# Experts of a two-layer trunk: order of the full-column products, a tenth weight block, and a pool for the first mixer's constants

## The chip, the cores and the metric

One core of one Trainium2 chip. The metric is the device time of one execution, in microseconds (us). The kernel before took 1505.41 us (median of 3 runs, 1500.89 to 1505.77).

## What is computed

Two layers over 512 tokens of width 1024, all in float32. Each has a mixer and then a mixture of 16 experts, in which every expert takes the 64 tokens with the highest affinity. Cut to what matters here:

```python
for layer in range(DEPTH):                     # DEPTH = 2; mixer 0: attention + pooling, mixer 1: gated convolution
    ...
    h_lat = _post_norm(h_lat, m_lat[2] * y_lat, ln_mix_g[layer], ln_mix_b[layer])
    f_lat = _expert_choice_ffn(_modulate(h_lat, m_lat[3], m_lat[4]), w_router[layer],
                               w_exp_gate[layer], w_exp_up[layer], w_exp_down[layer])
    h_lat = _post_norm(h_lat, m_lat[5] * f_lat, ln_ffn_g[layer], ln_ffn_b[layer])

def _expert_choice_ffn(u, w_router, w_g, w_u, w_d):    # u: (1, 512, 1024), 16 experts
    b, n, _ = u.shape
    cap = CAPACITY_FACTOR * n // N_EXPERTS             # 64 rows per expert
    logits = jnp.einsum('bnd,de->ben', u, w_router, preferred_element_type=jnp.float32)
    aff = jax.nn.softmax(logits, axis=1)
    gate, idx = lax.top_k(aff, cap)
    bidx = jnp.arange(b)[:, None, None]
    xe = u[bidx, idx]
    hg = jnp.einsum('becd,edf->becf', xe, w_g)         # w_g, w_u, w_d: (16, 1024, 1024) float32 per layer
    hu = jnp.einsum('becd,edf->becf', xe, w_u)
    ye = jnp.einsum('becf,efd->becd', jax.nn.silu(hg) * hu, w_d) * gate[..., None].astype(u.dtype)
    return jnp.zeros_like(u).at[bidx, idx].add(ye)
```

The weights of the experts are 2 x 16 x 3 matrices of 4 MB, 403 MB, which are read from HBM once.

## The kernel before

The order of every engine's instructions is the order of the Python code; nothing reorders it.

**Weight blocks.** A weight block is a tile of 128 partitions x 16 KB (2 MB, half a matrix). There are eight in the pool `base` (tags B0 to B7) and, while experts run, a ninth in a pool of its own (`x8`, opened by `open_x8`, L831). `self.queue` lists all loads in the order of use. Whenever a step has read a block for the last time, `next_load(b)` (L213) pops the next item and issues its load into that block on SP's queue; the load waits there until the block's readers are done. In an expert 0 the blocks of the gate and up products are given back in halves (`next_half`, L226). Once the last down matrix of a layer has been popped, block 8 is not loaded again: it becomes `self.spare`, which holds two rows of layer-norm constants (`gb`, built by `ln_row`, L269, with 32 TensorE matmuls into `p_gb`).

**One expert** (L1335 to L1372). TensorE's stationary operand is 64 columns wide in the products, since an expert has 64 tokens, so two matmuls for the two halves of the 1024 outputs run side by side in the two column halves of the array (64x512 each; the profile calls them 128\*64). A product `p_g`, `p_u` or `p_d` is 32 of these (`product`, L1289, two weight blocks of 16). The other steps of TensorE use all 128 columns: `gather` (`p_ga`, L1277, 32 matmuls: a selection matrix times H collects half of the features for the next pair of experts), the four transposes of the hidden rows (`p_t`, L1359), one matmul for the next selection matrix (`p_sb`, L1309, 16 rows deep) and `scatter` (`p_sc`, L1327: two matmuls per tile of 128 tokens, then two VectorE operations that add them into the accumulator `A`, L1330). The scatter belongs to the expert before, and is placed so:

```python
p_g = product("g", ...)            # 64-column
scatters(0)                        # tiles 0 and 1 of the expert before: 4 matmuls
p_u = product("u", ..., lambda: scatters(2))   # tiles 2 and 3, between the two halves of up
gather(g, 4 * (e % 2), 4 * (e % 2) + 4)        # not in experts 14 and 15
p_t, hT; st = scatter_sel(e)       # transposes, their copy, p_sb
p_d = product("d", ...)
```

In expert 15 the two halves of the scatter are in the middle of gate and behind it, and its down product is another routine (`out_mm`, L1384). PSUM has four banks with the tag `sc`, and one each with `g`, `u`, `d` and `tr`; gather, scatter, `p_sb` and `p_gb` use `sc`, the transposes `tr`.

**Around it.** `cst` holds all constants (1025 columns), among them the rotary tables and two tables that the first mixer alone reads; `condp` the conditioning vector padded with zeros to 32 columns. `x_load` (L837) reads x into H near the end of attention, and `load_gates` (L415) reads two bias rows at the start of layer 1's mixer; both go through POOL's queue.

Of the kernel before, what the change touches and what calls it, by code (L numbers as in the profile page):

```python
# [51 lines left out]
NCONST = _const_layout()  # L52


def _const_array():
# [7 lines left out]
    put("tri", np.triu(np.ones((P, P))))  # L63
    t = np.arange(S)
# [5 lines left out]
    put("cos", np.concatenate([cos, cos], -1).reshape(TT, P, HD).transpose(1, 0, 2))  # L70
    put("sin", np.concatenate([-sin, sin], -1).reshape(TT, P, HD).transpose(1, 0, 2))
    put("iota", np.broadcast_to(np.arange(1, CAP + 1), (P, CAP)))
    put("slot1", (np.arange(P) % CAP) + 1)
    sb = np.zeros((P, P))
    sb[0::32] = 1
    put("selb", sb)
    iv = np.ones((4, 16))
# [5 lines left out]
    put("inv", np.broadcast_to(iv, (P, 4, 16)))  # L83
    return a
# [101 lines left out]
class Trunk:  # L186
# [127 lines left out]
    def mod_item(self, layer, i, misc, dve=False, pool=None, kp=0, bufs=2):  # L314
# [12 lines left out]
        def sums(k0, k1):  # L327
# [5 lines left out]
            for k in range(k0, k1):  # L333
                c = self.condp[:, k, 0:1]
# [12 lines left out]
        def both(i):  # L347
# [18 lines left out]
        def share(i):  # L366
# [10 lines left out]
            nc.gpsimd.tensor_tensor(W[:, i], W[:, i], self.condp[:, i, 0:1].to_broadcast([P, 512]), ALU.mult)  # L377
            c = self.condp[:, KH + i, 0:1]
# [8 lines left out]
        def second():  # L387
# [11 lines left out]
            sel = one.to_broadcast([P, P]) if dve else self.cv("selb")  # L399
# [15 lines left out]
    def load_gates(self, layer, m2b, eng=None):  # L415
# [4 lines left out]
        eng = eng or nc.gpsimd  # L420
# [15 lines left out]
    def run(self):  # L436
# [5 lines left out]
        self.condp = base.tile([P, KO, 32], F32, name="condp")  # L442
        self.identb = base.tile([NE, NE], BF16, name="identb")
# [42 lines left out]
    def layer0_mixer(self):  # L486
        nc, tc, ins, base = self.nc, self.tc, self.ins, self.base
        ident = self.cv("ident")
        with ExitStack() as st:
# [4 lines left out]
            wgrp = pool.tile([P, 4, P], F32, name="wgrp")  # L494
            identr = pool.tile([P, P], F32R, name="identr")
# [11 lines left out]
            with ExitStack() as s2:  # L507
# [30 lines left out]
                nc.sync.dma_start(self.cst, ins["cst"])  # L538
                nc.sync.dma_start(gq, ins["qkg"].broadcast_to([P, 2 * HD]))
# [13 lines left out]
                nc.gpsimd.tensor_copy(self.identb, self.cv("ident", NE)[:, 0:NE])  # L553
# [86 lines left out]
                cs = self.cv("cos").rearrange("p (t i) -> p t i", t=TT)  # L640
                sn = self.cv("sin").rearrange("p (t i) -> p t i", t=TT)
# [189 lines left out]
    def open_x8(self, layer):  # L831

        self.layer, self.spare, self.x8s = layer, None, ExitStack()
        self.x8 = self.x8s.enter_context(self.tc.tile_pool(name=f"x8_{layer}", bufs=1))
        self.next_load(8)

    def x_load(self):  # L837

        self.H = self.base.tile([P, TT, D], F32, tag="H", name="H")
        self.nc.gpsimd.dma_start(self.H, self.ins["x"])  # L840

    def attention(self, pool, ps, identr, kH, kL, v, pp, wgrp, qs, qm, ms, nmx, sm, ri, s_tile, pb_mm, pb_out, mod_steps):
# [14 lines left out]
        with tc.tile_pool(name="l0a", bufs=1) as wk:  # L857
# [16 lines left out]
            def pool_group(g):  # L874
# [12 lines left out]
                iv = self.cv("inv").rearrange("p (g i) -> p g i", g=4)[:, g]  # L887
# [305 lines left out]
    def topk(self, layer, aff, sp, free, steps):  # L1193
# [45 lines left out]
        nc.scalar.copy(self.slotb, pr)  # L1239
# [4 lines left out]
    def moe(self, layer):  # L1244
# [6 lines left out]
        with tc.tile_pool(name=f"ex{layer}", bufs=2) as wk:  # L1251
# [18 lines left out]
            def gather(g, j0, j1, e0=0, e1=2):  # L1270
# [3 lines left out]
                pg = self.bank(shape=(P, j1 - j0, n), name="p_ga")  # L1274
# [60 lines left out]
            for e in range(NE):  # L1335
# [10 lines left out]
                scatters(2 if e == NE - 1 else 0)  # L1346
# [3 lines left out]
                p_u = product("u", lambda k: xe[k // KH][:, k % KH, e % 2], f"u{layer}_{e}", None if e == NE - 1 else lambda: scatters(2), e == 0)  # L1350
# [10 lines left out]
                nc.vector.tensor_copy(hT, p_t)  # L1361
                st = scatter_sel(e)
# [323 lines left out]
```

## Time and profile before

| | us |
|---|---|
| median of 3 runs | 1505.41 |
| the profiled execution's own time | 1505.35 |
| its span, first to last instruction | 1503.5 |
| layer 0 up to its first expert product | 0 to 308.7 |
| experts of layer 0, gate of expert 0 to down of expert 15 | 308.7 to 756.5 |
| end of layer 0, mixer 1, routing | 756.5 to 1021.7 |
| experts of layer 1 | 1021.7 to 1475.4 |
| last layer norm and output | 1475.4 to 1503.5 |

Over the span TensorE is busy 92%, VectorE 48%, ScalarE 22%, GpSimd 18%. A row of the timeline is a run of like instructions: start, length, engine, line, operation, out<-in, shape, count, and in brackets how long the engine stood idle before it and what released it. In rows of PE the length reaches to the modelled end of the last matmul, so it overlaps the next row a little; the distance from start to start is the time that a step takes. PEld is the weight load of TensorE. The chain of waits gives the pieces that ended last, in order of time. The DMA share is that of the core's 16 DMA engines.

### The profile page before, as it was taken

Reading aid. Unit: us, or ns where it says so; the run is one execution under the profiler, and the core shown is the slowest. Engines: PE = TensorE matmul, PEld = TensorE weight load, DVE = VectorE, ACT = ScalarE, POOL = GpSimd, SP = SyncE. Lnnn points to the kernel's source line nnn. Section 1 sums busy time; section 2 is a strip of 40 time slices with the busy share of each in tenths; the row PEclk is TensorE's granted clock in tenths of the full one; section 3 lists DMA queues with packets and bytes.
Section 4 is the critical chain, followed back from the end, with each engine's and each line's share of the span. In section 5 each row is a group of like instructions: output and inputs, shape, how many; then the busy total and the mean of one; then the engine's idle time right before and its main releaser. Section 6 shows DMA issues by size and latency. Waiting matters only on the chain. (4 is left out here: it accounts for less than half of the span.)

```text
span 1503.5 us, 17507 instructions
## 1 busy us (share of the span) xinstructions
PE 1390.6 (92%) x7162; PEld 770.3 (51%) x7162; DVE 718.3 (48%) x1157; ACT 336.6 (22%) x661; POOL 270.7 (18%) x240
## 2 busy tenths in 40 slices
PE   7989998799999999999959999979999999999993
PEld 5865556654444444444348787765444444444432
DVE  3674868813433433433476788570333343343346
ACT  3455650311011111111043222231101101101104
POOL 1421638530000000000065344022000000000003
PEclk9989998799999999999989999979999999999996
DMA  9437246879999999999942654747999999999981
GB/s 373 161 112 304 109 168 234 326 286 416 427 427 426 427 426 426 426 427 427 416 185 89 239 197 168 280 172 298 426 428 426 426 428 428 425 428 425 427 352 56
DMA packets 42319, 490.35 MB, mean 326 GB/s; under 512 B 4736, under 2 KB 5056, under 8 KB 12928
## 3 DMA queue, kind: packets, MB, share of 16 engines
q1 hardware_dynamic: 41712, 486.10, 78.4%
q0 software_dynamic: 384, 2.88, 0.5%
q8 instruction: 56, 0.92, 0.3%
q10 hardware_dynamic: 144, 0.26, 0.0%
q14 instruction: 23, 0.19, 0.0%
HBM read 487.13 MB, written 2.10 MB: 325 GB/s over the span
## 5 line engine op out<-in xcount | busy, mean ns | idle before, releaser
L1330 DVE SCALAR_TENSOR_TENSOR A<-p_sc_sc,gates,A 128x512 f32<-128x512 f32 x240 | 163.6, 745 | 178.9 <-PE p_sc_sc L1327 178.9
L1299 PE MATMUL p_u<-blk,xe 128*64 128x512 f32 x1024 | 232.9, 598 | 0.0
L1299 PE MATMUL p_g<-blk,xe 128*64 128x512 f32 x1024 | 226.1, 593 | 2.2 <-ACT xe L1286 2.2
L1299 PE MATMUL p_d<-blk,hT 128*64 128x512 f32 x960 | 212.6, 595 | 14.2 <-DVE hT L1361 14.2
L1299 PEld LDWEIGHTS p_g<-blk,xe 128*64 128x64 f32 x1024 | 73.0, 137 | 146.4 <-issue 141.2
L1379 POOL COPY m5c<-m5b 64x256 f32<-64x256 f32 x8 | 3.2, 397 | 773.8 <-PE p_ga_sc L1277 773.5
L1299 PEld LDWEIGHTS p_d<-blk,hT 128*64 128x64 f32 x960 | 66.3, 137 | 143.0 <-issue 119.9
L1299 PEld LDWEIGHTS p_u<-blk,xe 128*64 128x64 f32 x1024 | 68.4, 136 | 134.3 <-issue 121.2
L1277 PEld LDWEIGHTS p_ga_sc<-sel,H 128*128 128x128 f32 x1024 | 120.8, 197 | 25.8 <-issue 23.5
L1286 ACT ACTIVATE xe<-p_ga_sc,FG 128x128 f32<-128x128 f32 x128 | 48.2, 456 | 368.8 <-PE p_ga_sc L1277 368.8
L1277 PE MATMUL p_ga_sc<-sel,H 128*128 128x128 f32 x1024 | 126.8, 284 | 1.4 <-ACT slotb L1239 1.4
L1318 DVE TENSOR_TENSOR rows<-p_d,m5b 128x512 f32<-128x512 f32 x30 | 20.7, 691 | 195.9 <-PE p_d L1299 195.9
L1321 ACT CAST yp<-rows 64x512 fp32r<-64x512 f32 (+1 forms) x68 | 40.3, 593 | 258.5 <-DVE rows L1318 257.7
L1327 PE MATMUL p_sc_sc<-yp,st 128*128 128x512 f32 x240 | 71.9, 421 | 0.0
L242 POOL TENSOR_TENSOR blk<-blk,blk 128x1024 fp32r<-128x1024 f32 (+1 forms) x25 | 59.0, 2380 | 67.2 <-ACT blk L241 67.2
L1361 DVE COPY hT<-p_t_tr 128x512 f32<-128x512 f32 x32 | 22.2, 692 | 99.0 <-PE p_t_tr L1359 99.0
L1327 PEld LDWEIGHTS p_sc_sc<-yp,st 128*128 128x128 f32 x240 | 40.4, 188 | 54.0 <-issue 37.3
L246 PE MATMUL p_c_sc<-blk,blk 128*128 128x512 f32 x168 | 67.8, 404 | 0.0
L248 PE MATMUL p_c_sc<-blk,blk 128*128 128x512 f32 x168 | 66.4, 395 | 0.0
L247 PE MATMUL p_c_sc<-blk,blk 128*128 128x512 f32 x168 | 66.2, 394 | 0.0
L1322 DVE TENSOR_TENSOR yp<-rows,yp 64x512 fp32r<-64x512 f32 (+1 forms) x68 | 45.7, 672 | 25.3 <-ACT yp L1321 24.2
L1345 ACT ACTIVATE sg<-p_g 128x512 f32<-128x512 f32 x32 | 19.1, 598 | 154.5 <-PE p_g L1299 154.5
(394 smaller groups left out, 2006.0 us busy)
## 6 DMA issues: line engine op xcount, KB each, us to landing
blk<-wg SPq DMA_DIRECT2D x62, 2048.0 KB, 17.5
blk<-wu SPq DMA_DIRECT2D x58, 2048.0 KB, 17.0
blk<-wd SPq DMA_DIRECT2D x56, 2048.0 KB, 19.6
blk<-wmod SPq DMA_DIRECT2D x23, 2048.0 KB, 8.7
blk<-wci SPq DMA_DIRECT2D x8, 1536.0 KB, 12.2
blk<-wd SPq DMA_DIRECT2D x8, 1024.0 KB, 7.5
blk<-wu SPq DMA_DIRECT2D x16, 512.0 KB, 22.2
blk<-wdl SPq DMA_DIRECT2D x16, 512.0 KB, 10.2
```

The costliest lines, as they stand in the source:

```text
L242: (eng or nc.vector).tensor_tensor(lo, src, hi.bitcast(F32), ALU.subtract)
L246: mm(out, ah, bh, start=start, stop=False)
L247: mm(out, ah, bl, start=False, stop=False)
L248: mm(out, al, bh, start=False, stop=stop)
L1277: nc.tensor.matmul(pg[:, j - j0], H[:, t, j * P:(j + 1) * P], sels[g][:, t, e0:e1].rearrange("p e s -> p (e s)"), start=t == 0, stop=t == ...
L1286: nc.scalar.activation(o, pg[:, j - j0], AF.Identity, bias=self.FG[:, 1, j:j + 1], scale=self.FG[:, 0, j:j + 1])
L1299: nc.tensor.matmul(o[64 * hf:64 * hf + 64], lhs(k), W[:, kk, hf * 512:hf * 512 + 512], start=k == 0, stop=k == KO - 1)
L1321: nc.scalar.copy(yp[r, hf], ye[r])
L1322: nc.vector.tensor_tensor(yp[q, hf], ye[r], yp[r, hf].bitcast(F32), ALU.subtract)
L1327: nc.tensor.matmul(pp[hf], st[:, t * P:(t + 1) * P], yp[:, hf], start=True, stop=True)
L1330: nc.vector.scalar_tensor_tensor(a, pp[hf], self.gateT[:, t, e:e + 1], a, ALU.mult, ALU.add)
L1361: nc.vector.tensor_copy(hT, p_t)
```

## The change

In experts 0 to 14 both halves of the scatter leave the gate and up products: tiles 0 and 1 now stand between up and gather, tiles 2 and 3 between the transposes and `p_sb`. The gathers of the loop write to bank `g`, `p_sb` to bank `tr`. `p_sb` is 128 rows deep, with zeros in `slotb` below its 16 rows. A tenth block, 9, is opened beside block 8 in each layer's `x8` pool. To make room, the rotary tables and two more tables move to `cst0` in the first mixer's pool, with a load of their own; `condp` moves there too, filled by a VectorE copy from `cond`, which keeps its two columns; and the scratch for software DMA is cut to 256. `x_load` and `load_gates` of layer 1 issue from ScalarE's queue instead of POOL's.

```diff
@@ block, next_load @@
-        return (self.x8 if b == 8 else self.base).tile([P, n], dt, tag=f"B{b}" if isinstance(b, int) else b, name=f"blk{b}_{self.n}", bufs=1)
+        return (self.x8 if b in (8, 9) else self.base).tile([P, n], dt, tag=f"B{b}" if isinstance(b, int) else b, name=f"blk{b}_{self.n}", bufs=1)
...
-        if b == 8 and not any(it and it[0][:2] == f"d{self.layer}" for it in self.queue):
-            self.spare = self.block(b)
+        if b in (8, 9) and not any(it and it[0][:2] == f"d{self.layer}" for it in self.queue):
+            if b == 8:
+                self.spare = self.block(b)
             return
@@ open_x8 @@
         self.next_load(8)
+        self.next_load(9)
@@ constants: layout, run, layer0_mixer @@
-    for name, n in (("ident", P), ("tri", P), ("cos", TT * HD), ("sin", TT * HD), ("iota", CAP),
-                    ("slot1", 1), ("selb", P), ("inv", 4 * 16)):
+    for name, n in (("ident", P), ("tri", P), ("iota", CAP), ("slot1", 1)):
...
-        self.condp = base.tile([P, KO, 32], F32, name="condp")
-        self.identb = base.tile([NE, NE], BF16, name="identb")
+        self.cond = base.tile([P, KO, 2], F32, name="cond")
+        self.identb = base.tile([P, NE], BF16, name="identb")
...
-        self.slotb = base.tile([NE, S], BF16, name="slotb")
+        self.slotb = base.tile([P, S], BF16, name="slotb")
+        nc.gpsimd.memset(self.slotb, 0.0)
...
+            cst0 = pool.tile([P, NROPE + NSELB + NINV], F32, name="cst0")
+            self.selb = cst0[:, NROPE:NROPE + NSELB]
+            self.pinv = cst0[:, NROPE + NSELB:].rearrange("p (g i) -> p g i", g=4)
+            condp = self.condp = pool.tile([P, KO, 32], F32, name="condp")
+            nc.gpsimd.memset(condp, 0.0)
+            nc.vector.tensor_copy(condp[:, :, 0:2], self.cond)
...
                 nc.sync.dma_start(self.cst, ins["cst"])
+                nc.sync.dma_start(cst0, ins["cst0"])
@@ load_gates, x_load @@
-        eng = eng or nc.gpsimd
+        eng = eng or nc.scalar
...
-        self.nc.gpsimd.dma_start(self.H, self.ins["x"])
+        self.nc.scalar.dma_start(self.H, self.ins["x"])
@@ moe: gather, scatter_sel @@
-            def gather(g, j0, j1, e0=0, e1=2):
+            def gather(g, j0, j1, e0=0, e1=2, tag="sc"):
...
-                pg = self.bank(shape=(P, j1 - j0, n), name="p_ga")
+                pg = self.bank(tag, (P, j1 - j0, n), "p_ga")
...
-                pb = self.bank(name="p_sb")
-                nc.tensor.matmul(pb, self.identb[:, e:e + 1].to_broadcast([NE, P]), self.slotb, start=True, stop=True)
+                pb = self.bank("tr", name="p_sb")
+                nc.tensor.matmul(pb, self.identb[:, e:e + 1].to_broadcast([P, P]), self.slotb, start=True, stop=True)
@@ moe: the loop over the experts @@
-                scatters(2 if e == NE - 1 else 0)
+                if e == NE - 1:
+                    scatters(2)
...
-                p_u = product("u", lambda k: xe[k // KH][:, k % KH, e % 2], f"u{layer}_{e}", None if e == NE - 1 else lambda: scatters(2), e == 0)
+                p_u = product("u", lambda k: xe[k // KH][:, k % KH, e % 2], f"u{layer}_{e}", None, e == 0)
...
                 nc.vector.tensor_tensor(hid, sg, p_u, ALU.mult)
+
+                if e < NE - 1:
+                    scatters(0)
                 if g < NE // 2:
-                    gather(g, 4 * (e % 2), 4 * (e % 2) + 4)
+                    gather(g, 4 * (e % 2), 4 * (e % 2) + 4, tag="g")
...
                 nc.vector.tensor_copy(hT, p_t)
+                if e < NE - 1:
+                    scatters(2)
                 st = scatter_sel(e)
@@ kernel @@
-    nc = bacc.Bacc("TRN2", target_bir_lowering=False, num_devices=1)
+    nc = bacc.Bacc("TRN2", target_bir_lowering=False, num_devices=1, dynamic_dma_scratch_size=256)
```

TensorE in expert 1 of layer 0, before (`p_g`, `p_u`, `p_d`: products, `blk` their weight blocks; `p_sc`: scatter; `p_ga`: gather; `p_t`: transposes; x8: eight instructions in one row):

```order
L1299 MATMUL p_g<-blk_40_2215,xe 64x512 x8
L1299 MATMUL p_g<-blk_41_2217,xe 64x512 x8
L1327 MATMUL p_sc_sc<-yp,st 128x512 x4
L1299 MATMUL p_u<-blk_42_2342,xe 64x512 x8
L1327 MATMUL p_sc_sc<-yp,st 128x512 x4
L1299 MATMUL p_u<-blk_34_1890,xe 64x512 x8
L1277 MATMUL p_ga_sc<-sel,H 128x128 x16
L1359 MATMUL p_t_tr<-cst,rows 128x128 x4
L1309 LDWEIGHTS identb
L1309 MATMUL p_sb_sc<-slotb,identb 128x512
L1299 MATMUL p_d<-blk_35_1892,hT 64x512 x8
```

The same stretch now:

```order
L1312 MATMUL p_g<-blk_40_2220,xe 64x512 x8
L1312 MATMUL p_g<-blk_41_2222,xe 64x512 x8
L1312 MATMUL p_u<-blk_42_2224,xe 64x512 x8
L1312 MATMUL p_u<-blk_43_2349,xe 64x512 x8
L1340 MATMUL p_sc_sc<-yp,st 128x512 x4
L1290 MATMUL p_ga_g<-sel,H 128x128 x16
L1376 MATMUL p_t_tr<-cst,rows 128x128 x4
L1340 MATMUL p_sc_sc<-yp,st 128x512 x4
L1322 LDWEIGHTS identb
L1322 MATMUL p_sb_tr<-slotb,identb 128x512
L1312 MATMUL p_d<-blk_34_1798,hT 64x512 x8
```

Both rows of the scatter moved behind up; the second part of up reads a tenth block here (blk_43), where before block 34 had been loaded again for it.

VectorE in the same expert 1 (`rows<-sg,p_u`: hidden rows; `hT`: copy of the transposes; `A`: adds of the scatter; `st`: next selection), before:

```order
L1318 TENSOR_TENSOR rows<-p_d,m5b 128x512
L1322 TENSOR_TENSOR yp<-rows,yp 64x512 x2
L1330 SCALAR_TENSOR_TENSOR A<-p_sc_sc,gates,A 128x512 x8
L1354 TENSOR_TENSOR rows<-sg,p_u 128x512
L1361 COPY hT<-p_t_tr 128x512
L1311 TENSOR_SCALAR st<-p_sb_sc,cst 128x512
```

and now:

```order
L1331 TENSOR_TENSOR rows<-p_d,m5b 128x512
L1335 TENSOR_TENSOR yp<-rows,yp 64x512 x2
L1368 TENSOR_TENSOR rows<-sg,p_u 128x512
L1343 SCALAR_TENSOR_TENSOR A<-p_sc_sc,gates,A 128x512 x4
L1378 COPY hT<-p_t_tr 128x512
L1343 SCALAR_TENSOR_TENSOR A<-p_sc_sc,gates,A 128x512 x4
L1324 TENSOR_SCALAR st<-p_sb_tr,cst 128x512
```

Four of the eight adds now stand between the hidden rows and the copy `hT`, and four behind the copy.

TensorE at the end of layer 1, experts 14 and 15 (`p_gb`: the layer-norm constants), now:

```order
L1340 MATMUL p_sc_sc<-yp,st 128x512 x4
L1322 LDWEIGHTS identb
L1322 MATMUL p_sb_tr<-slotb,identb 128x512
L283 MATMUL p_gb_sc<-lnr,cst 128x128 x16
L1312 MATMUL p_d<-blk_236_7985,hT 64x512 x8
L1312 MATMUL p_d<-blk_237_7995,hT 64x512 x8
L1312 MATMUL p_g<-blk_238_8008,xe 64x512 x8
```

Before, `p_gb` stood behind `p_sb` of expert 15, just ahead of the last down product; with ten blocks the turns of block 8 are others, and it is spare one expert earlier. In layer 0 `p_gb` stays in expert 15.

## Rows read from the trace of the kernel before

**Rows 1.** The page: the span.

```profile
span 1503.5 us, 17507 instructions
```

**Rows 2.** Windows: stretch, length, PE, PEld, DVE, ACT, POOL busy (count), clock, DMA share, GB/s.

```profile
345.00:750.00 405.00, 397.60 (x1988) 169.54 (x1986) 142.80 (x210) 45.86 (x95) 1.59 (x4) 1.00 1.01 426
1003.00:1023.00 20.00, 13.91 (x80) 11.88 (x81) 10.55 (x27) 5.55 (x10) 16.92 (x14) 0.58 0.69 281
```

**Rows 3.** Timeline of PE over one expert of layer 0.

```profile
595.41 7.04 PE L1299 MATMUL p_g<-blk,xe 128*64 128x512 f32 x32
602.38 1.19 PE L1327 MATMUL p_sc_sc<-yp,st 128*128 128x512 f32 x4
603.50 3.65 PE L1299 MATMUL p_u<-blk,xe 128*64 128x512 f32 x16
607.08 1.20 PE L1327 MATMUL p_sc_sc<-yp,st 128*128 128x512 f32 x4
608.21 3.65 PE L1299 MATMUL p_u<-blk,xe 128*64 128x512 f32 x16
611.80 3.84 PE L1277 MATMUL p_ga_sc<-sel,H 128*128 128x128 f32 x32
615.47 0.60 PE L1359 MATMUL p_t_tr<-cst,rows 128*128 128x128 f32 x4
616.01 0.38 PE L1309 MATMUL p_sb_sc<-slotb,identb 16*128 16x512 bf16 x1
616.86 0.65 PE L1299 MATMUL p_d<-blk,hT 128*64 128x512 f32 x2 [0.47 <-DVE hT L1361]
```

**Rows 4.** Timeline of the same expert: VectorE, and the gather's weight loads.

```profile
607.62 2.73 DVE L1330 SCALAR_TENSOR_TENSOR A<-p_sc_sc,gates,A 128x512 f32<-128x512 f32 x4 [1.38 <-PE p_sc_sc L1327]
...
611.97 0.69 DVE L1354 TENSOR_TENSOR rows<-sg,p_u 128x512 f32<-128x512 f32 x1 [1.63 <-issue]
616.11 0.69 DVE L1361 COPY hT<-p_t_tr 128x512 f32<-128x512 f32 x1 [3.45 <-PE p_t_tr L1359]
...
611.80 3.65 PEld L1277 LDWEIGHTS p_ga_sc<-sel,H 128*128 128x128 f32 x32 [0.81 <-issue]
```

**Rows 5.** Timeline of PE in mixer 1: matmuls of 256 columns in a row.

```profile
790.26 0.28 PE L246 MATMUL p_c_g<-blk,blk 128*128 128x256 f32 x1
790.38 0.28 PE L247 MATMUL p_c_g<-blk,blk 128*128 128x256 f32 x1
```

**Rows 6.** The chain that ended last, experts 14 and 15 of layer 1: start, length, piece.

```profile
1437.52 0.70 DVE rows L1354
...
1439.70 7.09 PE p_d L1299 x32
1446.79 3.43 PE p_g L1299 x16
...
1451.35 3.58 PE p_g L1299 x16
...
1463.20 0.70 DVE rows L1354
...
1464.92 3.77 PE p_gb_sc L277 x32
```

**Rows 7.** Timeline of PE in layer 0: second half of expert 15's gate product.

```profile
739.21 3.65 PE L1299 MATMUL p_g<-blk,xe 128*64 128x512 f32 x16
```

**Rows 8.** Line L210, one load each: issued at (layers 0, 1), then issue to landing.

```profile
L210 SPq DMA_DIRECT2D blk<-wg x1: 328/328/328, 705.7 to 705.7; - x1
...
DMA to landing us min/median/max: 24.5/24.5/24.5
...
L210 SPq DMA_DIRECT2D blk<-wg x1: 328/328/328, 1417.7 to 1417.7; - x1
...
DMA to landing us min/median/max: 25.1/25.1/25.1
```

**Rows 9.** Timeline of ScalarE: a DMA issued from its queue.

```profile
1496.52 0.37 ACTq L1516 DMA_DIRECT2D out<-H  x1
```

More of the change, by code (lines that the diff above doesn't have):

```diff
@@ L52 @@
 NCONST = _const_layout()
+NROPE, NSELB, NINV = 2 * TT * HD, P, 4 * 16
 def _const_array():
@@ L63, in _const_array, with _const0_array @@
     put("tri", np.triu(np.ones((P, P))))
+    put("iota", np.broadcast_to(np.arange(1, CAP + 1), (P, CAP)))
+    put("slot1", (np.arange(P) % CAP) + 1)
+    return a
+def _const0_array():
     t = np.arange(S)
@@ L69, in _const_array @@
     cos, sin = np.cos(ang).astype(np.float32), np.sin(ang).astype(np.float32)
[L70 to L74, printed above, removed]
+    tab = np.stack([np.concatenate([cos, cos], -1), np.concatenate([-sin, sin], -1)])
+    sb = np.zeros((P, P), np.float32)
     sb[0::32] = 1
-    put("selb", sb)
-    iv = np.ones((4, 16))
+    iv = np.ones((4, 16), np.float32)
     for g, w in enumerate(WIN):
@@ L82, in _const_array @@
             iv[g, 8 + i] = 1.0 / (w - 1 - i)
-    put("inv", np.broadcast_to(iv, (P, 4, 16)))
-    return a
+    return np.concatenate([tab.reshape(2, TT, P, HD).transpose(2, 0, 1, 3).reshape(P, NROPE), sb,
+                           np.broadcast_to(iv.reshape(1, NINV), (P, NINV))], 1)
 _V = {}
@@ L125, in _pack @@
     o["cst"] = _const_array()
+    o["cst0"] = _const0_array()
     vec = np.empty((P, NVEC), np.float32)
@@ L333, in sums @@
             for k in range(k0, k1):
-                c = self.condp[:, k, 0:1]
+                c = self.cond[:, k, 0:1]
                 if k < kp:
@@ L356, in both @@
             for k in range(KH):
-                nc.gpsimd.tensor_tensor(W[:, k], W[:, k], self.condp[:, k, 0:1].to_broadcast([P, 512]), ALU.mult)
+                nc.gpsimd.tensor_tensor(W[:, k], W[:, k], self.cond[:, k, 0:1].to_broadcast([P, 512]), ALU.mult)
                 if k:
                     nc.gpsimd.tensor_tensor(W[:, 0], W[:, 0], W[:, k], ALU.add)
-                c = self.condp[:, KH + k, 0:1]
+                c = self.cond[:, KH + k, 0:1]
                 if k:
@@ L376, in share @@
                 return
-            nc.gpsimd.tensor_tensor(W[:, i], W[:, i], self.condp[:, i, 0:1].to_broadcast([P, 512]), ALU.mult)
-            c = self.condp[:, KH + i, 0:1]
+            nc.gpsimd.tensor_tensor(W[:, i], W[:, i], self.cond[:, i, 0:1].to_broadcast([P, 512]), ALU.mult)
+            c = self.cond[:, KH + i, 0:1]
             if i:
@@ L398, in second @@
             p_b = misc("mod_b")
-            sel = one.to_broadcast([P, P]) if dve else self.cv("selb")
+            sel = one.to_broadcast([P, P]) if dve else self.selb
             if g == 0:
@@ L453, in run @@
         self.smc = base.tile([P, 4], F32, name="smc")
-        self.slotb = base.tile([NE, S], BF16, name="slotb")
+        self.slotb = base.tile([P, S], BF16, name="slotb")
+        nc.gpsimd.memset(self.slotb, 0.0)
         self.lnr = base.tile([64, P], F32, name="lnr")
-        nc.gpsimd.memset(self.condp, 0.0)
-        nc.scalar.activation(self.condp[:, :, 0:2], self.vv("cond").rearrange("p (k s) -> p k s", s=2), AF.Silu)
+        nc.scalar.activation(self.cond, self.vv("cond").rearrange("p (k s) -> p k s", s=2), AF.Silu)
         nc.scalar.preload_act_table_set("natural_log_exp_and_others")
@@ L552, in layer0_mixer @@
                     nc.gpsimd.tensor_copy(kL[96:98, kv, :], ones[96:98, :].to_broadcast([2, KEYS]))
-                nc.gpsimd.tensor_copy(self.identb, self.cv("ident", NE)[:, 0:NE])
+                nc.gpsimd.tensor_copy(self.identb, self.cv("ident")[:, 0:NE])
                 nc.gpsimd.tensor_copy(identr, ident)
@@ L638, in layer0_mixer @@
                           for i in range(2))
-                cs = self.cv("cos").rearrange("p (t i) -> p t i", t=TT)
-                sn = self.cv("sin").rearrange("p (t i) -> p t i", t=TT)
+                cs, sn = (cst0[:, a * TT * HD:(a + 1) * TT * HD].rearrange("p (t i) -> p t i", t=TT) for a in range(2))
                 half = lambda e: slice(32 * e, 32 * e + 32)
@@ L886, in pool_group @@
                 nc.vector.scalar_tensor_tensor(pd, src, 1.0 / w, pin, ALU.mult, ALU.subtract)
-                iv = self.cv("inv").rearrange("p (g i) -> p g i", g=4)[:, g]
+                iv = self.pinv[:, g]
                 for a, n, i0 in ((0, w // 2, 0), (S - w // 2 + 1, w // 2 - 1, 8)):
@@ L1238, in topk @@
             nc.tensor.transpose(pr[:, t * P:(t + 1) * P], self.slotT[:, t, :], ident)
-        nc.scalar.copy(self.slotb, pr)
+        nc.scalar.copy(self.slotb[:NE], pr)
         for b in free:
```

## The prediction

> **What bounds the kernel now.** I read the windows by stage first, then the timeline of one expert, the chain of waits, and last the landing of single loads. [...] So two limits lie close together. TensorE's is the step of one expert: 21.45 us from gate to down (595.41 to 616.86) [rows 3] and 7.09 for down [rows 6], about 28.5. That of the loads is six blocks of 2048 KB: 2.097 MB at 426 GB/s is 4.92 us, times six 29.5. The loads are the slower by 1 us per expert, but nine blocks are full when a layer begins, and that stock is eaten up slowly. How much is left at the end is the margin of expert 15's second gate half: in layer 0 it lands at 705.7 + 24.5 = 730.2 and is read from 739.21, 9.0 us later; in layer 1 it lands at 1442.8 and is read from 1451.35, 8.5 us later [rows 6 to 8]. TensorE sets the end, and may become faster by 8 to 9 us per layer before the loads do.
>
> What TensorE loses at a change between 64 and 128 columns is in the rows too. An unbroken half product takes 3.43 us, one behind a scatter 3.58 [rows 6]; a group of four scatter matmuls takes 1.12 or 1.13 from start to start [rows 3]. So a break costs 1.13 + 0.15 = 1.28. The four matmuls have 512 columns each; 256 columns follow each other every 0.12 us [rows 5], so 512 take 0.24 and four 0.96. An expert has two such breaks.
>
> **The change, part by part.** (1) *The scatter leaves gate and up.* From gate to gather 16.39 us pass now (595.41 to 611.80) [rows 3]. Without breaks there are four halves of 3.43 and 0.11 to leave the products (602.38 - 595.41 = 6.97 against 6.86): 13.83. That saves 2.56. The first group now stands ahead of the gather, both on 128 columns: between 0.96 (pure) and 1.28 (as a break); I take 1.00, since rows 5 show such matmuls without a change of width. Saved: 1.56.
>
> (2) *The second group stands between the transposes and* `p_sb`. From transposes to down 1.39 us pass (615.47 to 616.86), 0.54 of it the transposes; for the rest TensorE mostly waits for the copy `hT`, 0.69 [rows 3, 4]. Now: 0.54, the group 1.00, `p_sb` 0.25 (between 0.24 by rows 5 and 0.38 by rows 3), 0.15 to go back to 64 columns, 1.94 in all: 0.55 more, bounds 0.35 and 0.96. Some 0.7 of the group is covered by the copy. Together 1.01 saved per expert (bounds 0.32 and 1.25). Experts 1 to 13 have a scatter and a gather: 13 x 1.01 = 13.1 us per layer.
>
> (3) *VectorE's queue.* The four adds of the first group now stand ahead of the copy `hT`, which down waits for. They are 2.73 us behind 0.69 for the hidden rows [rows 4]; hidden rows start 0.17 after up ends, so the adds end at 3.6, and the transposes end at 1.00 + 3.67 + 0.54 = 5.2. The gather hides them. Expert 14 has no gather: from the hidden rows to down 2.18 us pass now (1437.52 to 1439.70) [rows 6], then 0.69 + 2.73 + 0.69 + 0.25 = 4.36. It loses 2.2 there and saves 2.56: 0.3 gained. So layer 0 gains 13.4.
>
> (4) `p_gb` *goes from expert 15 to expert 14 in layer 1.* It needs four `sc` banks, which the adds of the second group give back only after the copy, at 0.69 + 2.73 + 0.69 = 4.1 and then 0.68 apart: 4.8 to 6.8. Its last quarter (3.77 / 4 = 0.94) [rows 6] ends at 7.8, 5.6 later than down starts now. With the 2.56 saved expert 14 loses 3.1. In expert 15 `p_gb` ends at 1464.92 + 3.77 = 1468.69; without it down could start 2.18 behind 1463.20, 3.3 us earlier [rows 6]. Layer 1: 13.1 - 3.1 + 3.3 = 13.3.
>
> (5) *The tenth block.* It gains nothing where TensorE sets the end; it holds the loads off. Each layer's loads run one block ahead, if that block is read in time in which the DMA engines aren't full: in 1003 to 1023, ahead of layer 1's experts, their share is 0.69 [rows 2]. The margin grows by 4.92, to 13.9 and 13.5. The need is 13.4 in layer 0 and 13.1 - 3.1 = 10.0 at that place in layer 1: both just fit. Without it the gain would stop at 9.0 and 8.5.
>
> [...]
>
> (6) *Constants, queues, pools.* One more DMA on SP at the start (0.33 each [rows 8]), a small copy ahead of the first matmuls; x and three bias rows now issue from ScalarE at 0.37 each [rows 9], x just ahead of attention's last exponentials, the others behind waits for GpSimd's last reads of H, with mixer 1's first copies queued behind them. Nothing to 2.0 us; I take 1.0. The gather in bank `g` has a whole down product for its evacuation: nothing.
>
> Sum: 13.4 + 13.3 - 1.0 = 25.7. The profiled execution took 1505.35 us (a span of 1503.5 [rows 1] and 1.85 around it), the median is 1505.41. 1505.35 - 25.7 = 1479.7, so **1480**. With the upper bound of 1.25, layer 0 stops at 13.9 and layer 1 reaches 16.3 - 3.1 + 3.3 = 16.5, and (6) at nothing: 1475.
>
> **The rivals.** *The breaks are not a matter of width* (1498): the scatter's weight loads show wherever it stands, and a group costs 1.28 anywhere. Then 0.32 per expert is saved: 4.5 and 4.4, less 2: 1498. The gather speaks against it: its 32 weight loads (3.65) and 32 matmuls (3.84) start together and lie side by side [rows 3, 4]. [...]
>
> *The tenth block comes late* (1485): its space is freed only when the layer's experts run, and it does not do what it is there for. The gain stops at 9.0 in layer 0 and at 8.5 + 3.3 in layer 1, less 1: 19.8, 1485.5. Against it: the DMA engines have room ahead of the experts [rows 2].
>
> [...]
>
> *No gain* (1505): block 9's load stands in SP's queue ahead of others; if its space comes free some 25 us late, the loads behind it lose what TensorE wins.
>
> *Slower: the copy* `hT` *waits for the adds* (1522). They have from 0.86 (0.17 + 0.69) to 5.2, 1.09 each, against 0.68 now [rows 4]. Beyond that, each 0.1 costs 0.4 per expert, 10.4 over 26 experts. To be slower by more than 0.3% the add must reach 1.38; at 1.5 it is 0.41 x 4 x 26 = 43 us, 1522. Nothing in the rows makes an add twice as long.
>
> **How the numbers follow.** Forecast 0.67 (its own range 1475 to 1488), late block 0.12, breaks stay 0.10, loads set the pace 0.03, no gain 0.05, slower 0.03. The range from 1474 to 1492 holds the forecast with the bounds of its unknown costs and the late block; what lies outside it has about 0.2. A measurement of this kernel tells 0.3%, 4.5 us, from no change. Faster 0.92, same 0.05, slower 0.03.
>
> **What would show it.** Right: gate and up as one run of 13.8 us; the first scatter to the gather 1.0; transposes to down 1.9; an expert step near 27.4; the margin of expert 15's second gate half above zero, but below 4; `p_gb` in expert 14 of layer 1, and its down some 8 us behind the hidden rows. Wrong: a scatter group of 1.28 in its new places; TensorE waiting for a block from expert 12 on; `hT` waiting for an add in experts 1 to 13; a tenth load that is issued behind the first gate product.

## The result, and the profile after

The changed kernel takes 1482.63 us (median of 4 runs, 1479.12 to 1488.14), the kernel before 1504.8 beside it: a ratio of 0.9861, 95% interval 0.9825 to 0.9897, so 1.0 to 1.8% faster. The forecast was 1480 in a range from 1474 to 1492. The medians lie 22.2 us apart. The profiled execution is the shortest of the four, 1479.12 us, so the 26.2 us of its table are more than the median gains. By stages, from first instruction to first instruction (the down product of expert 15 begins at 1468.61 in layer 1 of the kernel before; the table of stages further up counts its experts to 1475.4):

| us | before | after | difference |
|---|---|---|---|
| up to the first expert product of layer 0 | 308.73 | 307.72 | -1.01 |
| from there to expert 15's down, layer 0 | 447.81 | 434.54 | -13.27 |
| from there to layer 1's first expert product | 265.20 | 263.97 | -1.23 |
| from there to expert 15's down, layer 1 | 446.87 | 434.73 | -12.14 |
| from there to the end of the span | 34.89 | 36.34 | +1.45 |
| span | 1503.5 | 1477.3 | -26.2 |

In this execution the sum is near the forecast (25.7), and the two expert stages are near their 13.4 and 13.3. The profile shows that they are so for other reasons. First the page: the span, and the group of the up products with its idle time; 5.8 us of it now end with the landing of a load, where before there was none.

```profile
span 1477.3 us, 17436 instructions
...
L1312 PE MATMUL p_u<-blk,xe 128*64 128x512 f32 x1024 | 226.3, 593 | 5.8 <-DMA blk<-wu 5.8
```

Next the timeline of PE over one expert of layer 0, which answers to [rows 3], and VectorE beside it, which answers to [rows 4].

```profile
582.79 7.04 PE L1312 MATMUL p_g<-blk,xe 128*64 128x512 f32 x32
589.66 7.04 PE L1312 MATMUL p_u<-blk,xe 128*64 128x512 f32 x32
596.63 1.20 PE L1340 MATMUL p_sc_sc<-yp,st 128*128 128x512 f32 x4
597.66 3.73 PE L1290 MATMUL p_ga_g<-sel,H 128*128 128x128 f32 x32
601.23 0.60 PE L1376 MATMUL p_t_tr<-cst,rows 128*128 128x128 f32 x4
601.59 1.18 PE L1340 MATMUL p_sc_sc<-yp,st 128*128 128x512 f32 x4
602.61 0.38 PE L1322 MATMUL p_sb_tr<-slotb,identb 128*128 128x512 bf16 x1
602.92 1.51 PE L1312 MATMUL p_d<-blk,hT 128*64 128x512 f32 x6
```

```profile
596.80 0.69 DVE L1368 TENSOR_TENSOR rows<-sg,p_u 128x512 f32<-128x512 f32 x1 [10.23 <-PE p_u L1312]
597.41 2.72 DVE L1343 SCALAR_TENSOR_TENSOR A<-p_sc_sc,gates,A 128x512 f32<-128x512 f32 x4
601.87 0.69 DVE L1378 COPY hT<-p_t_tr 128x512 f32<-128x512 f32 x1 [1.74 <-PE p_t_tr L1376]
602.48 2.06 DVE L1343 SCALAR_TENSOR_TENSOR A<-p_sc_sc,gates,A 128x512 f32<-128x512 f32 x3
```

From gate to gather 14.87 us pass (597.66 - 582.79; forecast 14.83), the first group takes 1.03, and from transposes to down it is 1.69 (602.92 - 601.23; forecast 1.94). With 6.92 for down (the distance from down to the next gate) the step is 27.05, against 28.37 before: 1.32 saved, more than the forecast's upper bound of 1.25. The copy `hT` waits for the transposes alone; the adds ended 1.74 us earlier. So the slower rival did not come.

Now the end of layer 0, experts 14 and 15: PE's timeline, and the load of the second gate block of expert 15.

```profile
699.57 3.65 PE L1312 MATMUL p_u<-blk,xe 128*64 128x512 f32 x16 [0.67 <-DMA blk<-wu]
704.48 3.65 PE L1312 MATMUL p_u<-blk,xe 128*64 128x512 f32 x16 [1.26 <-DMA blk<-wu]
...
724.11 3.65 PE L1312 MATMUL p_g<-blk,xe 128*64 128x512 f32 x16
```

```profile
L215 SPq DMA_DIRECT2D blk<-wg x1: 328/328/328, 684.9 to 684.9; - x1
...
DMA to landing us min/median/max: 39.2/39.2/39.2
```

That block lands at 684.9 + 39.2 = 724.1 and is read from 724.11. The margin, 9.0 us before [rows 7, 8] and 13.9 by the forecast with a tenth block, is used up to the last tenth, and TensorE has waited for loads already: 2.6 us in three waits in layer 0 and 3.2 in layer 1.

The chain that ended last shows the same in layer 1 (start, length, piece): loads, then expert 14 with `p_gb`, then its down.

```profile
1323.80 39.76 DMA blk<-wg
...
1363.57 0.02 SPq L215
...
1363.62 39.16 DMA blk<-wu
...
1402.83 3.68 PE p_u L1312 x16
...
1406.58 0.69 DVE rows L1368
...
1411.22 3.83 PE p_gb_sc L283 x32
1415.05 7.02 PE p_d L1312 x32
```

Down stands 8.47 us behind the hidden rows (1415.05 - 1406.58), where the forecast's sum had 7.8. What was not forecast stands in expert 15 of layer 1. TensorE waits twice there, as it does in layer 0, and here the windows (columns as in [rows 2]) show that the next product runs at a granted clock of 0.67 (5.2 us, where the same 32 matmuls take 3.5 from start to start in layer 0):

```profile
1439.22 0.66 PE L1376 MATMUL p_t_tr<-cst,rows 128*128 128x128 f32 x4 [0.85 <-DVE rows L1368]
1440.66 0.38 PE L1322 MATMUL p_sb_tr<-slotb,identb 128*128 128x512 bf16 x1 [0.78 <-DVE hT L1378]
1440.96 5.36 PE L1408 MATMUL p_d<-blk,hT 128*64 128x256 f32 x32
```

```profile
1438.40:1440.96 2.56, 0.96 (x5) 0.49 (x5) 1.38 (x2) 0.00 (x0) 0.00 (x0) 1.00 0.66 264
1440.96:1446.15 5.19, 5.19 (x33) 3.12 (x34) 0.75 (x1) 0.00 (x0) 0.00 (x0) 0.67 0.07 28
```

So three questions were open: whether the loads set the pace at the end of a layer, which of the two groups brings the 1.32, and what the move of `p_gb` and the fall of the clock cost.

### The profile page after: what moved, and what is told of

Its sections match the earlier page's. It is cut to its first block, busy times and chain, and to the rows that moved or that the text cites. A ratio compares the mean times of both kernels' runs of the same rounds, so it can differ in the third digit from the quotient of the medians.

```text
span 1477.3 us, 17436 instructions
## 1 busy us (share of the span) xinstructions
PE 1370.3 (93%) x7162; PEld 775.5 (52%) x7162; DVE 713.6 (48%) x1158; ACT 336.4 (23%) x661; POOL 269.5 (18%) x237
## 5 line engine op out<-in xcount | busy, mean ns | idle before, releaser
L1312 PE MATMUL p_u<-blk,xe 128*64 128x512 f32 x1024 | 226.3, 593 | 5.8 <-DMA blk<-wu 5.8
L1368 DVE TENSOR_TENSOR rows<-sg,p_u 128x512 f32<-128x512 f32 x32 | 22.0, 687 | 325.8 <-PE p_u L1312 315.7
L1312 PEld LDWEIGHTS p_u<-blk,xe 128*64 128x64 f32 x1024 | 72.5, 137 | 153.9 <-issue 140.6
L1299 ACT ACTIVATE xe<-p_ga_g,FG 128x128 f32<-128x128 f32 x112 | 42.2, 457 | 306.8 <-PE p_ga_g L1290 306.8
L1290 PEld LDWEIGHTS p_ga_g<-sel,H 128*128 128x128 f32 x896 | 104.2, 192 | 3.1 <-issue 0.8
L1290 PE MATMUL p_ga_g<-sel,H 128*128 128x128 f32 x896 | 104.7, 275 | 0.0
L349 DVE SCALAR_TENSOR_TENSOR rows<-blk,cond,rows 128x512 f32<-128x512 f32 x49 | 54.2, 1106 | 1.5
```

The costliest lines, as they stand in the source:

```text
L349: nc.vector.scalar_tensor_tensor(a, W[:, k], c, a, ALU.mult, ALU.add)
L1290: nc.tensor.matmul(pg[:, j - j0], H[:, t, j * P:(j + 1) * P], sels[g][:, t, e0:e1].rearrange("p e s -> p (e s)"), start=t == 0, stop=t == ...
L1299: nc.scalar.activation(o, pg[:, j - j0], AF.Identity, bias=self.FG[:, 1, j:j + 1], scale=self.FG[:, 0, j:j + 1])
L1312: nc.tensor.matmul(o[64 * hf:64 * hf + 64], lhs(k), W[:, kk, hf * 512:hf * 512 + 512], start=k == 0, stop=k == KO - 1)
```

## Do the loads set the pace?

**The new order with nine blocks** (`order_only`)

```diff
         self.next_load(8)
-        self.next_load(9)
```

> The new order of the products with nine blocks, the tenth is never opened. Theory L (from expert 13 on the loads set the pace): every layer's load stream is one block of 4.92 us later. Layer 0 ends 4.9 later than in the changed kernel, in layer 1 the last load lands 9.8 later, of which some 3 us are slack behind the last down product: a span of about 1484 (1482 to 1488), TensorE waits for blocks earlier and for 7 us or more per layer. Theory P (TensorE still sets the end, the 2.6 and 3.2 us of waiting for blocks are incidental): a span within 2 us of the changed kernel's 1477.3. By the prediction's step 5 the gain stops at 9.0 and 8.5 us: about 1487.

The page, the group of the up products:

```profile
L1311 PE MATMUL p_u<-blk,xe 128*64 128x512 f32 x1024 | 227.3, 594 | 13.8 <-DMA blk<-wu 13.8
```

1487.86 us, ratio 0.9899 (0.9884 to 0.9914). Layer 0 takes 439.51 us from its first expert product to expert 15's down, 4.97 more than with ten blocks: one block of 4.92. TensorE waits 6.7 us for blocks in layer 0 and 7.1 in layer 1, from expert 11 on. This is theory L; up to expert 10 TensorE's step is 27.05 as in the changed kernel, so the time can't come from there. The prediction's step 5, which has the gain stop at 9.0 and 8.5 us, gives 1505.4 - 17.5 = 1487.9 (one more with the loss of its step 6). The expert stages themselves gain 8.3 and 7.7 us.

**The tenth block with the old order** (`block_only`)

```diff
-                if e == NE - 1:
-                    scatters(2)
+                scatters(2 if e == NE - 1 else 0)
...
-                p_u = product("u", ..., None, e == 0)
+                p_u = product("u", ..., None if e == NE - 1 else lambda: scatters(2), e == 0)
...
-                if e < NE - 1:
-                    scatters(0)
...
-                if e < NE - 1:
-                    scatters(2)
```

(`gather` and `p_sb` are back in bank `sc` too.)

> The tenth block, pools and queues as changed, but the order of products, scatter, gather and p_sb as before. Both theories: TensorE sets the end with the old step of 28.37 us, so no gain in the experts; p_gb of layer 1 stands in expert 14 (longer by 3.8), expert 15 is shorter by 3.3 and its down product runs at the lower clock (1.8 longer): 1502 to 1508. If the tenth block brought time by itself: 1495 or less.

1503.55 us, ratio 0.9997 (0.9988 to 1.0006): no difference. The step is 28.36, nothing waits for a block, and expert 15's second gate half lands 13.2 us ahead of its use in layer 0 (9.0 before, 13.9 forecast). The tenth block alone gives 0, the new order alone 1.0%, both together 1.4%. Since this kernel has all else that was changed, it prices the constants, queues and pools too: with the move of `p_gb`, which comes to nothing here (expert 14 is 3.12 longer, expert 15 up to its down 3.25 shorter), they cost between -1.8 and 0.9 us. The lower clock that I expected in expert 15 did not come: here `p_sb` is in bank `sc` and does not wait. In layer 1 TensorE waits there too, 0.85 us ahead of the transposes and 0.57 ahead of down.

**One load less** (`one_load_less`)

```diff
             name, src, n = it
+            if name.endswith("_10_1") and name[0] == "d":
+                n = 256
...
+                    twice = name[0] == "d" and name.endswith("_10")
+                    if twice and h:
+                        W = self.w[f"{name}_0"][0]
...
```

> The changed kernel, but in expert 10 of each layer the second block of down is loaded with 128 KB instead of 2048, and the down product reads the first block twice (another result, the same matmuls). The loads behind it come 4.6 us earlier. Theory L: the waits for blocks (2.6 us in layer 0, 3.2 in layer 1, and some 0.2 for each restart) are gone: 5 to 7 us less, a span of 1470 to 1472. Theory P: within 1.5 us of the changed kernel.

The page, the group of the up products:

```profile
L1316 PE MATMUL p_u<-blk,xe 128*64 128x512 f32 x1024 | 225.2, 592 | 0.0
```

1476.09 us, ratio 0.9809 (0.9793 to 0.9826): 6.5 less than the changed kernel, and no wait for a block in either layer. Expert 13 of layer 0 is back at 27.05, expert 14 takes 25.20 instead of 27.57. So the waits were real, and TensorE would use an earlier load. How much of the 6.5 is waiting and how much falls of the clock, which differ from one execution to the next, the medians can't say. The median is some 3 us above what theory L had (a span of 1470 to 1472 and 1.85 around it); the profiled execution, with a span of 1479.2, has two falls of the clock as described below (`p_gb` takes 6.77 us in expert 15 of layer 0 and 7.05 in expert 14 of layer 1, instead of 3.83), which no theory had counted.

**Less work for TensorE** (`less_pe`)

```diff
-                if e < NE - 1:
+                if e == NE - 2:
                     scatters(2)
```

> The changed kernel without the second scatter group (tokens 256 to 511) in experts 1 to 13 of both layers: these matmuls and adds are left out, so A lacks those sums. TensorE has 13 x 1.03 = 13.4 us less to do per layer. Theory L (the loads set the end): layer 0 gains nothing, layer 1 at most the 3 us of slack behind its last load: a span of 1474 to 1477, and 12 us or more per layer of waiting for blocks. Theory P (TensorE sets the end): 24 to 27 us less, 1450 to 1453.

1482.66 us, ratio 0.9854 (0.9837 to 0.9871), the changed kernel's time. But this does not decide between L and P, as I had meant it to, since TensorE's step did not become shorter. PE's timeline of an expert without the second group:

```profile
602.80 0.60 PE L1376 MATMUL p_t_tr<-cst,rows 128*128 128x128 f32 x4
604.18 0.38 PE L1322 MATMUL p_sb_tr<-slotb,identb 128*128 128x512 bf16 x1 [0.78 <-DVE hT L1378]
604.49 7.09 PE L1312 MATMUL p_d<-blk,hT 128*64 128x512 f32 x32
```

From transposes to down it is 1.69 with the group and without it (604.49 - 602.80). Where the group stood, `p_sb` now waits for the copy: it writes to bank `tr`, which the copy reads. With `p_sb` in that bank the second group is free.

## Which group brings the 1.32 us?

**The first group back, the second moved** (`second_only`)

```diff
-                if e == NE - 1:
-                    scatters(2)
+                scatters(2 if e == NE - 1 else 0)
...
-                if e < NE - 1:
-                    scatters(0)
```

> The changed kernel with the first scatter group back between gate and up; the second stays between the transposes and p_sb. Theory S (the second group costs nothing where it now stands, since the copy hT and p_sb take those 1.69 us anyway): gate to up 8.09, transposes to down 1.69, a step of 27.35 us, so that 1.0 of the 1.32 saved per expert comes from the second group. By the prediction's steps 1 and 2 the second group alone saves 1.28 - 0.55 = 0.73: a step of 27.64. Either way the loads have a margin or nearly so: little or no wait for blocks, within 3 us of the changed kernel apart from falls of the clock.

The step is 27.39, gate to up 8.09, transposes to down 1.70 (607.36 - 605.66 in the rows of PE's timeline below). Theory S.

```profile
605.66 0.60 PE L1373 MATMUL p_t_tr<-cst,rows 128*128 128x128 f32 x4
606.02 1.17 PE L1340 MATMUL p_sc_sc<-yp,st 128*128 128x512 f32 x4
607.05 0.38 PE L1322 MATMUL p_sb_tr<-slotb,identb 128*128 128x512 bf16 x1
607.36 7.09 PE L1312 MATMUL p_d<-blk,hT 128*64 128x512 f32 x32
```

The time is 1480.46 us, ratio 0.984 (0.9821 to 0.986), no more than that of the changed kernel, and TensorE waits for no block. The 0.34 us by which the whole change is quicker per expert are mostly spent waiting for loads: from the first expert product to expert 15's down the profile has 435.65 us in layer 0 and 434.75 in layer 1, against 434.54 and 434.73. So the move of the first group brings 1.1 us in one layer and nothing in the other.

**The second group back, the first moved** (`one_break`)

```diff
-                p_u = product("u", ..., None, e == 0)
+                p_u = product("u", ..., None if e == NE - 1 else lambda: scatters(2), e == 0)
...
-                if e < NE - 1:
-                    scatters(2)
                 st = scatter_sel(e)
```

> The changed kernel with the second scatter group back between the halves of up, p_sb still in bank tr. If a change of width costs 0.15 on each side: up is 1.28 longer, transposes to down back from 1.69 to about 1.35, a step of 27.05 + 0.95 = 28.0 us, so that of the 1.32 saved per expert 0.95 belongs to the second group and 0.35 to the first. TensorE then sets the end again, no wait for blocks: about 9.4 us more per layer, near 1496. If a scatter group costs the same anywhere: a step of 26.7 to 27.1 and no change of time.

1511.34 us, ratio 1.0048 (1.0033 to 1.0063): 0.3 to 0.6% slower than before the change. The step is 28.33, not 28.0: transposes to down stays at 1.69, with `p_sb` waiting 0.78 as above. With that the move of the first group gains 0.04. Expert 14 loses more: the adds stand ahead of the copy and no gather hides them, `p_sb` waits 2.50 for it in layer 1, and `p_gb` and down behind it take 7.20 and 8.39 us; in the changed kernel they take 3.83 and 7.09, at a granted clock of 1.00 (from 1411.2 to 1421.9 us).

**The same with** `p_sb` **in bank** `sc` (`first_only_sc`)

```diff
-                pb = self.bank("tr", name="p_sb")
+                pb = self.bank(name="p_sb")
```

> As one_break (only the first group is moved), but p_sb in bank sc. Theory S: transposes to down back at 1.39, a step of 28.05 us, 0.3 less than the 28.33 of one_break: bank tr costs 0.3 where no scatter group covers it. Rival (the 1.69 of one_break has another cause than the bank): 28.33 again. Time 1495 to 1503, as experts 14 still wait for the adds.

PE's timeline of an expert of layer 0:

```profile
610.99 0.60 PE L1376 MATMUL p_t_tr<-cst,rows 128*128 128x128 f32 x4
611.42 0.38 PE L1322 MATMUL p_sb_sc<-slotb,identb 128*128 128x512 bf16 x1
612.37 7.09 PE L1312 MATMUL p_d<-blk,hT 128*64 128x512 f32 x32 [0.57 <-DVE hT L1378]
```

Transposes to down 1.38, a step of 28.02: the bank costs 0.31 where no group covers it. 1491.54 us, ratio 0.9913 (0.9891 to 0.9935), less than expected, since expert 14 lost 0.5 (26.17 against 25.66) and not 2.2.

## `p_gb`, two waits, and the clock

`p_gb` **of layer 1 in expert 15 again** (`gb_last`)

```diff
-                if self.spare and not gb:
+                if e == NE - 1 and not gb:
```

> The changed kernel with p_gb of layer 1 in expert 15, behind p_sb, as in layer 0. Theory K (without p_gb TensorE idles twice ahead of the last down product, and its granted clock falls there, which costs 1.8 us): expert 14 is 3.8 us or more shorter, expert 15 has its down 3.8 later but at a clock of 1.00 (3.5 us instead of 5.3): 2 to 3 us faster, a span near 1475. The prediction's step 4 (the move to expert 14 gains 0.2): 0 to 0.5 slower, and the last down product at 5.3 as now.

1483.89 us, ratio 0.9865 (0.9842 to 0.9888), the changed kernel's time, and a miss for theory K: the clock falls in spite of `p_gb`, now in both layers. Expert 15 of layer 0 in PE's timeline, and windows of it:

```profile
738.74 0.38 PE L1322 MATMUL p_sb_tr<-slotb,identb 128*128 128x512 bf16 x1 [0.78 <-DVE hT L1378]
739.05 6.86 PE L283 MATMUL p_gb_sc<-lnr,cst 64*128 64x128 f32 x32
745.84 5.55 PE L1408 MATMUL p_d<-blk,hT 128*64 128x256 f32 x32
```

```profile
735.00:738.50 3.50, 2.11 (x12) 0.77 (x9) 1.19 (x2) 0.00 (x0) 0.00 (x0) 1.00 1.03 410
738.50:745.00 6.50, 6.26 (x30) 5.95 (x30) 0.94 (x2) 1.79 (x3) 0.00 (x0) 0.57 1.04 422
745.00:750.00 5.00, 5.00 (x27) 3.01 (x27) 0.00 (x0) 1.88 (x2) 0.00 (x0) 0.53 1.02 425
```

The granted clock, 1.00 in the window ahead, is 0.57 and 0.53 in the two windows behind the two waits of 0.85 and 0.78; the same instructions of the changed kernel's layer 0 take 3.83 and 3.67 at 1.00. That is 3.03 + 1.88 = 4.9 us. It seems not to be there in each execution: the five go from 1479.38 to 1488.86 us, and over the whole span the granted clock is 0.952 and 0.953 in the two longest, 0.957 to 0.960 in the others.

`p_gb` **in the two waits** (`gb_fill`)

```diff
+                if e == NE - 1:
...
+                    self.ln_row(4 * layer + 2, g1[0], 1.0 if last else ALPHA)
                 p_t = self.bank("tr", (P, 4, P), "p_t")
...
                 nc.vector.tensor_copy(hT, p_t)
...
+                if e == NE - 1:
+                    self.ln_row(4 * layer + 3, g1[1], 1.0 if last else ALPHA)
                 st = scatter_sel(e)
-                if self.spare and not gb:
...
```

> As gb_last, but the two halves of p_gb in expert 15 of both layers stand where TensorE waits: one ahead of the transposes (0.85 us of waiting for the hidden rows), one behind them (0.78 for the copy hT). Theory L: nothing in layer 0, whose last down product already ends 0.4 us behind its last load, and up to 0.5 in layer 1 (last landing 1442.84 plus 0.45): a span of 1474 to 1475. Theory P: 0.85 less per layer than gb_last, near 1473.3.

Expert 15 of layer 1, PE's timeline and a window of it:

```profile
1433.55 2.05 PE L283 MATMUL p_gb_sc<-lnr,cst 64*128 64x128 f32 x16
1435.53 0.66 PE L1380 MATMUL p_t_tr<-cst,rows 128*128 128x128 f32 x4
1436.12 2.05 PE L283 MATMUL p_gb_sc<-lnr,cst 64*128 64x128 f32 x16
1438.10 0.39 PE L1322 MATMUL p_sb_tr<-slotb,identb 128*128 128x512 bf16 x1
1438.42 3.67 PE L1409 MATMUL p_d<-blk,hT 128*64 128x256 f32 x32
```

```profile
1433.50:1438.40 4.90, 4.90 (x39) 4.23 (x37) 1.38 (x2) 1.99 (x4) 0.00 (x0) 1.00 0.99 394
```

TensorE is busy without a gap at a clock of 1.00. 1474.32 us (1472.77 to 1474.87), ratio 0.9801 (0.9786 to 0.9816): faster than both kernels, and the runs lie within 2.1 us instead of 9. It is 9.6 us below the kernel with `p_gb` in one piece. The waits are 1.63 us per layer, 3.3 in all; the rest I put down to falls that don't come, which is a conclusion from the spread and the profiles, not a measurement. L and P are not told apart by its span of 1473.1.

`p_sb` **of expert 15 in bank** `sc` (`sb_sc_last`)

```diff
-                pb = self.bank("tr", name="p_sb")
+                pb = self.bank("sc" if e == NE - 1 else "tr", name="p_sb")
```

(with `p_gb` in expert 15 of both layers)

> As gb_last, but p_sb of expert 15 is in bank sc again, so that it does not wait for the copy hT, and p_gb follows it at once, as before the change. Theory W (the clock falls where TensorE waits twice, 0.85 and 0.78 us, ahead of p_gb): no fall, p_gb at 3.8 and the last down product at 3.5 to 3.7 in both layers, runs that lie within 4 us of each other, near 1475. Rival (the falls have nothing to do with the second wait): p_gb at 6.5 to 7 or a last down product above 5 in at least one layer, runs spread over 1479 to 1489 as in gb_last.

Expert 15 of layer 1 in PE's timeline:

```profile
1434.17 0.66 PE L1376 MATMUL p_t_tr<-cst,rows 128*128 128x128 f32 x4 [0.85 <-DVE rows L1368]
1434.67 0.38 PE L1322 MATMUL p_sb_sc<-slotb,identb 128*128 128x512 bf16 x1
1434.98 3.83 PE L283 MATMUL p_gb_sc<-lnr,cst 64*128 64x128 f32 x32
1438.74 3.67 PE L1408 MATMUL p_d<-blk,hT 128*64 128x256 f32 x32
```

1477.52 us (1475.22 to 1478.72), ratio 0.9817 (0.9796 to 0.9838): no fall, and a narrow spread, by one wait less. That is as theory W has it, though two places without a fall could be chance. Over the profiles of this study, expert 15 has both waits at 14 places (seven kernels, two layers) and a fall behind them at 5 (the last down product takes 5.36 to 5.92 us instead of 3.67, and `p_gb`, where it stands ahead of it, 6.50 to 6.86 instead of 3.83); at the 12 places without the wait of `p_sb` there is none. But these two waits are not the only ones with a fall behind them: in expert 14 of layer 1, where seven kernels have `p_gb`, it takes 7.05, 7.19 and 7.20 us in three, in `one_load_less` (the granted clock is 0.51 there) and `less_pe` behind four waits of 0.15 to 0.28 us and in `one_break` behind one of 2.50. The changed kernel has the four short waits too, and no fall there (3.83 us). What tells the places with a fall from the others stays open.

**Halves in expert 0's down** (`gb_fill_half`)

```diff
-                    split_y(product("d", lhs, f"d{layer}_{e}"), yp, self.m5b)
+                    split_y(product("d", lhs, f"d{layer}_{e}", None, e == 0), yp, self.m5b)
```

(on top of the kernel with `p_gb` in the two waits)

> As gb_fill, and expert 0 gives back the blocks of its down product in halves too, as it does those of gate and up. The DMA engines then start again 1.7 us earlier in expert 0 (they stand at a share of 0.82 in 330 to 340 us of the changed kernel). Theory L: each layer's loads end up to 1.7 us earlier, and the layer with them until TensorE binds: 1.5 to 3 us less than gb_fill, a span of 1471 to 1473. Theory P: no change against gb_fill.

1474.79 us, ratio 0.98 (0.9784 to 0.9815): nothing against 1474.32, and a miss for theory L. TensorE still waits 2.5 and 3.4 us for blocks, as with `p_gb` in the two waits alone (3.2 and 3.4). Counted from the layer's first expert product, expert 15's second gate half lands 0.95 us earlier in layer 0 and 0.06 in layer 1 (TensorE's last wait for a block, in expert 14, ends 0.91 and 0.04 earlier: 396.72 us against 397.63, and 396.90 against 396.94), and in layer 0 the other kernels with ten whole blocks differ by as much among themselves (416.35 to 417.44 us). Why it is not the 1.7 us that was expected stays open.

## Why the forecast was right, and where it was not

- **What bounds the kernel**: right. The loads were 8 to 9 us ahead of TensorE's needs, and beyond that the gain stops, as with nine blocks. The 426 GB/s that give a block its 4.92 us are those of the first line of [rows 2]; in the changed kernel it is 427 GB/s from 345 to 715 us, and the whole blocks issued from 600 to 700 us land 4.89 to 4.92 us apart. The step before is 28.37, not 28.5: the 7.09 for down is the length of the row, and from its start to the next gate it is 6.92.
- **Step 1, gate and up**: right: 14.87 against 14.83, a group in its new place 1.03 against 1.00. Why a group costs more between products (the 1.28 worked out from [rows 3, 6]) than beside full-width work (1.03), no run shows; the rows show only that it does.
- **Step 2, transposes to down**: the term that was mis-sized. The forecast's 1.94 has "some 0.7 of the group" covered by the copy. All of it is: 1.69 with and without the group, because `p_sb` in bank `tr` has to wait for the copy anyway. That bank, which I costed at nothing, costs 0.31 where no group stands. The rest came with the gather, which takes 3.57 behind the group instead of 3.67. In all 1.32 for 1.01. Of this the second group brings 0.98, for which steps 1 and 2 have 1.28 - 0.55 = 0.73, and the first 0.34, for which step 1 has 1.28 - 1.00 = 0.28. The whole new order with `p_sb` in bank `sc` was not run.
- **Step 3**: right. The adds are off the path in experts 1 to 13. For expert 14 the forecast was 0.3 gained (its terms, 2.56 and 2.18, give 0.38); without waits for blocks it is 0.46 (25.20 against 25.66, one load less).
- **Bank** `tr` **in experts 0 and 15**: not in the forecast. No second group stands there, so `p_sb` waits: 0.3 us in each expert 0, 0.8 in expert 15 of layer 0, and 0.3 in that of layer 1.
- **Step 4,** `p_gb`: forecast -3.1 and +3.3. Expert 14 takes 31.70. Less the 1.94 of waiting for blocks in it, and some 0.4 that the halves of up lose by starting anew behind these waits (gate to transposes 17.24, one load less 14.87), it is 3.7 more than the 25.67 before. Expert 15 gains 2.9 up to its down, the wait of `p_sb` included. Behind it the clock falls and takes 1.7 in the profiled execution: a loss of 2.5 instead of a gain of 0.2.
- **Step 5, "both just fit"**: wrong, though it left the sum right. A saving of 1.32 needs 13 x 1.32 = 17.2 us, more than the 13.9 of the margin. TensorE waits from expert 13 on, which I had named as a sign against the forecast. The gain of a layer is what the loads allow. Its sign at expert 15's second gate half, a margin above 0 and below 4, reads 0.0 us in layer 0 and 4.1 in layer 1. That the tenth block is loaded in time was right: its effect in layer 0 is 4.97, a full block.
- **Step 6**: forecast a loss of 1.0. The kernel with the old order puts it, with the move of `p_gb`, between a gain of 1.8 and a loss of 0.9. The 2.2 us won ahead of layer 0's and layer 1's experts in the profiled execution are not shown to come from the change: the first expert product of the 12 profiled executions of code that is the same up to there, save the tenth block, starts anywhere from 306.58 to 310.52.

So that the time came out so near is in part luck, through errors that cancel: 0.31 more per expert than forecast, which the loads did not let through, and the waits for a bank and the clock, against 2.2 us ahead of the experts that no run attributes. The forecast's mechanism, that breaks cost 1.28 and full-width neighbours 1.00 (measured 1.03), and that loads stop the gain, stands.

## What to carry to other kernels

When a stage has two limits that lie 4% apart, work out both and give the smaller of the two gains; here either part of the change alone gives at most 1.0%. Work moved off a path should go where its engine waits, and the place is found by taking the work out: if the time from one fixed point to the next stays the same (here 1.69 us from transposes to down, with the second group and without it), it is free there. A PSUM bank that two steps share can be a wait as real as a data dependence (here 0.78 us for `p_sb`, and 0.31 more from transposes to down), and here a wait of 0.78 us for a bank had 4.9 us of loss behind it where the clock fell.

## What was not expected of the hardware

- Two waits of TensorE, 0.85 and 0.78 us, with 0.66 us of transposes between them, are followed by a granted clock of 0.53 to 0.67 at some places and not at others. The cost is 1.7 us where only the last down product follows and 4.9 where `p_gb` stands ahead of it. The executions of the changed kernel spread over 9 us, those of the kernel with the waits filled over 2.1; that the falls are the reason is likely but not shown, since each kernel has the profile of one execution only.
- The loads that TensorE waits for were issued 39.2 us before they land, eight times the 4.9 by which one lands behind another; in the chain above the load of 1363.62 is issued just when another one lands (1323.80 + 39.76). In the experts of the changed kernel there are never more than eight of them under way. That is the program's doing: in the trace SP's loads raise eight semaphores in turn, and SP waits for a load's semaphore before it issues the next load with it. From 600 to 715 us 23 of SP's 32 waits end with the landing of an earlier load (92.6 of 109.0 us, the longest 4.6); from 345 to 500 us none does, and SP waits for TensorE. So a block that is given back late in a layer waits not only for its readers but also for an earlier load. What this costs no run shows; the DMA engines are full meanwhile, with a share of 1.01 from 345 to 715 us.
